# A hybrid encoder on one core: the first norm by square root and one Newton step, its first tiles reordered, and the last two tiles of the final norm woven

## The chip, the cores and the metric

The kernel runs on one core of a Trainium2 chip. The metric is the device time of one execution in microseconds (us); lower is better. Five engines work from queues of their own, each in order: TensorE (PE; its weight loads are listed as PEld), VectorE (DVE), ScalarE (ACT), GpSimd (POOL) and SyncE (SP, which here only issues transfers). Tiles lie in SBUF; TensorE writes its results to PSUM.

## The reference

Two layers work on 1024 tokens of width 1024. Layer 0 mixes by neighbourhood attention, layer 1 by grouped-query attention. Each layer then adds a gated per-layer embedding, and a last RMS norm ends the trunk.

```python
def rms_norm(x, g):
    xf = x.astype(jnp.float32)
    y = xf * lax.rsqrt(jnp.mean(xf * xf, axis=-1, keepdims=True) + NORM_EPS)
    return (y * g.astype(jnp.float32)).astype(x.dtype)

def reference(x, p, norm_g, ...):
    for i in range(DEPTH):                                  # DEPTH = 2
        h = rms_norm(x, norm_g[i])
        y = mixer_a(h, ...) if i % 2 == 0 else mixer_b(h, ...)
        x = x + y
        g = jax.nn.sigmoid(rms_norm(x, ple_norm_g[i]) @ ple_w_gate[i])
        x = x + g * (p[i] @ ple_w_proj[i])
    return rms_norm(x, final_norm_g)
```

`mixer_a` projects h to q, k, v and a gate, attends over a window of 8 rows x 16 columns with a learned bias, multiplies by silu(gate) and projects again. `mixer_b` does the like with normalised and rotated q and k over all tokens.

## The kernel before

**Tiles and numbers.** The 1024 tokens are eight tiles of 128 (`NT`). A product in float32 accuracy is three TensorE products: each operand is split in a high part and a low part (`wh`, `wl` for weights, `HTh`, `HTl` for the normalised and transposed tokens), and `split3` (through `mm`, line 305) adds high times high, high times low and low times high. The high part is an ACT copy, the low part a DVE subtraction.

**Weights.** `WQ` walks a list of units of 128 x 1024 numbers (512 KB). `stage` has SP issue the next load into one of two staging tiles `wstage` (line 203), as long as no more than two units are ahead of the split. `pump` copies the high part on ACT (line 220) and leaves the low part (line 221, DVE) to the next `settle`. At most `WSLOTS` = 4 split units live at a time. A pump that isn't forced waits for a few pumps after a load. The list begins with av0, av1 (the first quarter of V's weights), aqk0, aqk1.

**The start of layer 0** (`mixer_a`, the stretch behind `e2`). SP loads tile 0, the gain broadcast to all 128 partitions, tile 1, the two V units and tiles 2 to 7. For a tile t, `square(t)` (ACT, line 723) sums the squares, `newton` (DVE) makes the reciprocal root by an integer seed and three Newton steps, `scale(t)` multiplies the tile by root and gain (line 739 on DVE for tiles 0, 1, 2, 4, 6; lines 741 and 742 on ACT and POOL for 3, 5, 7), and `ht(t)` transposes it on TensorE in two halves of four blocks (line 430), which ACT copies to HTh (line 431) and DVE subtracts to HTl (line 432). `vs[t][0]` and `vs[t][1]` are the two halves of V's product for tile t, 12 matmuls each; ACT and DVE evacuate it (lines 590 and 591). The order of all that is written out by hand. Between t=0 and t=1, SP issues the mask and eight loads of the bias table into `U`; behind t=3, sixteen copies from `U` to `U2` (line 793). Then come the q and k products of head 0 (matmuls of 512 columns) and the attention loop, in which `mix` lays attention steps and dense products side by side by hand-set weights.

**The roots.** `rsqrt_ops` gives the list of tiny DVE operations of a reciprocal root: shift, multiply-add, a halving, and three Newton steps of two operations for one column or three for several. `newton`, `norms` and `finish_norm` (layer 1's q and k norms, spread over later slots by `post`) use it.

**The end** (`dense_phase(1)`, kind "ple", second half). For each tile, 24 matmuls of 512 columns fill a PSUM tile; `gated` takes tanh on ACT (line 1221) and two DVE operations (1222, 1223) that update X; ACT squares (1281); `norms` makes the root (414 and on), POOL scales the low half (419), DVE the high half (422), and SP stores the tile. The last tile is computed in two column halves (`halves`), its low half is scaled by ACT (421), and SP issues its two stores one after the other (1289, 1290). On DVE, `norms` of tile 6 comes before the `gated` operations of tile 7.

Of the kernel before, what the change touches and what calls it, by code (L numbers as in the profile page):

```python
# [11 lines left out]
F32 = mybir.dt.float32  # L12
# [9 lines left out]
NT = 8  # L22
KC = 8
# [4 lines left out]
BIG = 1e30  # L28
WSLOTS = 4
# [9 lines left out]
HOLD = 2  # L39
DP = 1  # L40
# [44 lines left out]
def lay_out(inp):  # L85
# [57 lines left out]
    def swap(v):  # L143
# [6 lines left out]
        "mask": mask, "rope": np.stack([cosT, sinT], axis=1),  # L150
    }
# [3 lines left out]
def trunk(ctx, tc, x, wts, rpb, gains, hgains, mask, rope, out):  # L155
# [21 lines left out]
    class Weights:  # L177
        def __init__(self):
# [13 lines left out]
            self.rest = None  # L192
            self.gate = None
# [13 lines left out]
        def pump(self, force=False):  # L207
# [13 lines left out]
            self.rest = lambda: dve.tensor_tensor(lo, s, hi, ALU.subtract)  # L221
# [90 lines left out]
    def rsqrt_ops(dst, ms, wk):  # L312
        n = dst.shape[1]
        mi = ms.bitcast(I32)
        y, a, h = wk[:, 0:n], wk[:, n:2 * n], wk[:, 2 * n:3 * n]
        yi = y.bitcast(I32)
        ops = [lambda: dve.tensor_scalar(yi, mi, 1, None, op0=ALU.logical_shift_right),
               lambda: dve.tensor_scalar(yi, yi, -1, 0x5F3759DF, op0=ALU.mult, op1=ALU.add),
               lambda: dve.tensor_scalar(h, ms, -0.5, None, op0=ALU.mult)]
        for i in range(3):  # L320
            to = dst if i == 2 else y
            if n == 1:
                ops += [lambda: dve.scalar_tensor_tensor(a, y, h, y, op0=ALU.mult, op1=ALU.mult)]
            else:
                ops += [lambda: dve.tensor_tensor(a, y, y, ALU.mult),
                        lambda: dve.tensor_tensor(a, a, h, ALU.mult)]
            ops += [lambda to=to: dve.scalar_tensor_tensor(to, a, 1.5, y, op0=ALU.add, op1=ALU.mult)]
        return ops

    def rsqrt(dst, ms, wk):  # L330
        for f in rsqrt_ops(dst, ms, wk):
            f()
# [50 lines left out]
    def proj_N(keys, t, ncol, alloc, evac, release=(), kstep=None):  # L383
# [5 lines left out]
        for k0, k1 in chunks(nk, kstep):  # L389
            def f(k0=k0, k1=k1):  # L390
                if k0 == 0:
                    st["ps"] = alloc()
                for k in range(k0, k1):
# [15 lines left out]
    def norms(sb, sq, ts, xns, xts, gt, final):  # L409
        n = len(ts)  # L410
        wk = sb.tile([128, 8], F32, name="wkn", bufs=2)
        st = sb.tile([128, 4], F32, name="stn", bufs=3)
        ms, r = st[:, 0:n], st[:, 2:2 + n]
        dve.scalar_tensor_tensor(ms, sq[:, 1, ts[0]:ts[0] + n], 1.0 / D, sq[:, 0, ts[0]:ts[0] + n], op0=ALU.mult, op1=ALU.add)
        rsqrt(r, ms, wk)
        for i in range(n):
            if final:
                if ts[i] < NT - 1:
                    pool.tensor_scalar(xns[i][:, :512], xts[i][:, :512], r[:, i:i + 1], None, op0=ALU.mult)
                else:  # L420
                    act.activation(xns[i][:, :512], xts[i][:, :512], AF.Copy, scale=r[:, i:i + 1])
                dve.scalar_tensor_tensor(xns[i][:, 512:], xts[i][:, 512:], r[:, i:i + 1], gt[:, 512:], op0=ALU.mult, op1=ALU.mult)
            else:
                dve.scalar_tensor_tensor(xns[i], xts[i], r[:, i:i + 1], gt, op0=ALU.mult, op1=ALU.mult)
# [138 lines left out]
    def mixer_a():  # L563
        with ExitStack() as es:
# [4 lines left out]
            psO = es.enter_context(tc.tile_pool(name="apo", bufs=2, space=PSUM))  # L569

# [14 lines left out]
            def v_items(qd, t):  # L585
# [6 lines left out]
                return [d[0] for d in proj_N(keys, t, 256, valloc, evac, release=keys if t == NT - 1 else ())]  # L592
# [119 lines left out]
            ini = e2.enter_context(tc.tile_pool(name="ini", bufs=1))  # L712
            X = [ini.tile([128, D], F32, name=f"X{t}") for t in range(NT)]
            gt = ini.tile([128, D], F32, name="gain")
# [10 lines left out]
            def newton(a, b):  # L725
                ms = stat[:, 1, a:b]
                return [lambda: dve.tensor_scalar(ms, stat[:, 0, a:b], 1.0 / D, EPS, op0=ALU.mult, op1=ALU.add)] \
                    + rsqrt_ops(stat[:, 2, a:b], ms, wk)

            def weave(ops, fs):  # L730
                per = -(-len(ops) // len(fs))
                for i, f in enumerate(fs):
                    for o in ops[i * per:(i + 1) * per]:
                        o()
                    f()

            def scale(t):
                if t % 2 == 0 or t == 1:
                    dve.scalar_tensor_tensor(X[t], X[t], stat[:, 2, t:t + 1], gt, op0=ALU.mult, op1=ALU.mult)
                else:  # L740
                    act.activation(X[t], X[t], AF.Copy, scale=stat[:, 2, t:t + 1])
                    pool.tensor_tensor(X[t], X[t], gt, ALU.mult)

            def ht(t):
                return [lambda c=c: to_ht(psT, t, X[t], (c,)) for c in range(2)]

            load(0)
            sync.dma_start(gt, bcast(gains, 0, D))
            load(1)
            WQ.stage(True)  # L750
            for t in range(2, NT):
                load(t)
            U = dram.tile([16, 8, 31, 24], F32, name="U")
            square(0)
            square(1)
# [19 lines left out]
            for t in range(1, NT):  # L775
# [3 lines left out]
                if t == 1:  # L779
                    square(7)  # L780
# [559 lines left out]
```

## Time and profile before

| | us |
|---|---|
| median of 3 runs (lowest to highest) | 1563.97 (1562.44 to 1564.62) |
| the profiled execution: its time | 1560.76 |
| its span, first to last instruction | 1558.9 |
| busy in it: TensorE / VectorE / ScalarE / GpSimd | 1519.0 / 1025.8 / 871.8 / 279.5 |

In the timeline a row has its start in us from the span's start, its duration, the engine, the line of the kernel, the operation, the tile written and the tiles read, their sizes and the count; a bracket gives the idle time of the engine just before it and what ended it. SPq is SyncE's transfer queue. Matmuls overlap, so the distance of two starts, not the duration, is what one costs.

### The profile page before, as it was taken

What the parts mean: (1) busy time and instruction counts of PE and PEld (TensorE: products, weight loads), DVE (VectorE), ACT (ScalarE), POOL (GpSimd) and SP (SyncE); (2) the same over time, 40 slices, a digit from 0 to 9 for tenths busy, and PEclk for the clock granted to TensorE, in tenths of its full rate; (3) what the DMA queues carried; (4) which work ended last, traced back from release to release, by engine and by line L of the source; (5) the groups of instructions that cost most, each with busy time, mean ns of one, the idle gap of its engine ahead of it and who ended that gap; (6) DMA issues with size and microseconds to landing.
All of it is one profiled execution on the core that took longest, in us unless ns stands there. A gap on an engine that the chain in (4) does not pass through costs nothing.

```text
span 1558.9 us, 24287 instructions
## 1 busy us (share of the span) xinstructions
PE 1519.0 (97%) x9048; PEld 1327.7 (85%) x9048; DVE 1025.8 (66%) x2062; ACT 871.8 (56%) x1744; POOL 279.5 (18%) x372
## 2 busy tenths in 40 slices
PE   6999999999999999999999999999999999999997
PEld 5888988988988788888988889989999888788886
DVE  6576477377477436648877787777877877625636
ACT  6465466376366622434466776766767777622422
POOL 2111121112112010000222132443131200000023
PEclk9999999999999999999999999999999999999999
DMA  8212122132122972142210111111111113651213
GB/s 274 78 41 75 44 89 79 35 95 82 35 85 83 336 260 68 54 141 94 76 49 21 39 38 55 45 38 50 56 33 42 61 55 117 225 200 54 75 55 128
DMA packets 89861, 138.84 MB, mean 89 GB/s; under 512 B 16912, under 2 KB 55952, under 8 KB 89744
## 3 DMA queue, kind: packets, MB, share of 16 engines
q1 hardware_dynamic: 85136, 122.62, 24.3%
q10 hardware_dynamic: 4608, 14.68, 2.6%
q8 instruction: 71, 1.16, 0.3%
q14 instruction: 46, 0.38, 0.1%
HBM read 104.65 MB, written 36.15 MB: 90 GB/s over the span
## 4 chain that ended last, share of the span: by engine, by line
PE 43%; DVE 6%; ACT 3%; issue 2%; ACTq 0%; DVEq 0%
PE d L305 23%; PE o L305 7%; PE t L1087 6%; PE s L305 6%; DVE PTl L1090 1%; DVE mn L1071 1%; ACT PTh L1089 1%; ACT P L1077 1%; PE t L430 1%; PE t L1041 0%; DVE QS L1051 0%; DVE wl L221 0%; DVE t L905 0%; DVE KB L982 0%; DVE qt L906 0%
## 5 line engine op out<-in xcount | busy, mean ns | idle before, releaser
L305 PE MATMUL d<-wh,HTh 128*128 128x256 f32 (+1 forms) x1096 | 372.6, 340 | 4.8 <-ACT HTh L431 2.1
L305 PE MATMUL d<-wh,HTl 128*128 128x256 f32 (+1 forms) x1096 | 365.9, 334 | 1.5 <-DVE HTl L432 1.5
L305 PE MATMUL d<-wl,HTh 128*128 128x256 f32 (+1 forms) x1096 | 365.2, 333 | 0.0
L1090 DVE TENSOR_TENSOR PTl<-t,PTh 128x512 fp32r<-128x512 f32 x256 | 164.5, 684 | 107.1 <-ACT PTh L1089 106.7
L305 PEld LDWEIGHTS d<-wh,HTh 128*128 128x128 f32 x1096 | 207.9, 190 | 28.2 <-ACT HTh L431 2.7
L305 PEld LDWEIGHTS d<-wh,HTl 128*128 128x128 f32 x1096 | 207.8, 190 | 24.0 <-DVE HTl L432 2.2
L305 PEld LDWEIGHTS d<-wl,HTh 128*128 128x128 f32 x1096 | 208.2, 190 | 21.4
L305 PE MATMUL d<-HTh,wh 128*128 128x512 f32 x504 | 206.0, 409 | 0.0
L305 PE MATMUL d<-HTh,wl 128*128 128x512 f32 x504 | 197.8, 392 | 0.0
L305 PE MATMUL d<-HTl,wh 128*128 128x512 f32 x504 | 197.7, 392 | 0.0
L1077 ACT ACTIVATE P<-s,mn 128x1024 f32<-128x1024 f32 x128 | 142.8, 1116 | 56.6 <-DVE mn L1071 55.7
L1089 ACT ACTIVATE PTh<-t 128x512 fp32r<-128x512 f32 x256 | 140.1, 593 | 45.8 <-PE t L1087 45.3
L1071 DVE TENSOR_REDUCE mn<-s 128x1 f32<-128x1024 f32 x128 | 154.9, 1210 | 11.9 <-PE s L305 11.8
L1087 PE MATMUL t<-ident,P 128*128 128x128 f32 x1024 | 136.9, 274 | 6.6 <-DVE PTl L1090 4.8
L221 DVE TENSOR_TENSOR wl<-wstage,wh 128x1024 fp32r<-128x1024 f32 x89 | 115.1, 1298 | 42.3 <-ACT wh L220 42.1
L305 PE MATMUL s<-KA,QS 128*128 128x512 f32 (+2 forms) x384 | 133.5, 402 | 0.0
L1087 PEld LDWEIGHTS t<-ident,P 128*128 128x128 f32 x1024 | 114.8, 140 | 21.7 <-DVE PTl L1090 15.8
L305 PE MATMUL s<-KB,QS 128*128 128x512 f32 (+2 forms) x384 | 121.8, 371 | 0.0
L305 PE MATMUL o<-PTh,V 128*128 128x256 f32 (+2 forms) x672 | 118.8, 287 | 1.5 <-DVE Y L446 0.9
L305 PE MATMUL o<-PTl,V 128*128 128x256 f32 (+2 forms) x672 | 119.3, 289 | 0.4 <-DVE PTl L684 0.3
L684 DVE TENSOR_TENSOR PTl<-t,PTh 128x384 fp32r<-128x384 f32 (+1 forms) x128 | 66.6, 521 | 76.1 <-ACT PTh L683 75.0
L305 PEld LDWEIGHTS d<-HTh,wl 128*128 128x128 f32 x504 | 94.6, 188 | 21.8
(179 smaller groups left out, 2483.6 us busy)
## 6 DMA issues: line engine op xcount, KB each, us to landing
wstage<-in_wts SPq DMA_DIRECT2D x92, 512.0 KB
X<-in_x SPq DMA_DIRECT2D x16, 512.0 KB
pp<-ppD SPq DMA_DIRECT2D x32, 256.0 KB
rb<-rD SPq DMA_DIRECT2D x56, 128.0 KB
ppD<-th SPq DMA_DIRECT2D x20, 256.0 KB
xD<-X SPq DMA_DIRECT2D x8, 512.0 KB
X<-xD SPq DMA_DIRECT2D x8, 512.0 KB
yD0h<-rb SPq DMA_DIRECT2D x14, 256.0 KB
```

The lines of the kernel that those rows point to most:

```text
L221: self.rest = lambda: dve.tensor_tensor(lo, s, hi, ALU.subtract)
L305: pe.matmul(ps, a, b, start=first, stop=last, skip_group_check=True)
L430: pe.transpose(ps[:, k], xn[:, (4 * c + k) * 128:(4 * c + k + 1) * 128], ident)
L684: dve.tensor_tensor(PTl[:, sl], ps[:, :m], PTh[:, sl], ALU.subtract)
L1071: dve.tensor_reduce(mn, ps, axis=AX.X, op=ALU.min)
L1077: act.activation(p, ps, AF.Exp, bias=mn, scale=-1.0, accum_out=RS[h, hf][:, t:t + 1])
L1087: pe.transpose(ps[:, i], p[:, k * 128:(k + 1) * 128], ident)
L1089: act.activation(PTh[:, ks, c], ps, AF.Copy)
L1090: dve.tensor_tensor(PTl[:, ks, c], ps, PTh[:, ks, c], ALU.subtract)
```

## The change

1. **Layer 0's norm.** `square(t)` is followed by a square root on ACT (`root`), a reciprocal on DVE and one Newton step, per tile. The gain comes as a 4 KB array laid out by the host (`gain0`, 128 x 8), loaded over ACT's queue and spread over the partitions by eight TensorE transposes into a PSUM tile `gain`. All scales run on DVE; tiles 0 and 1 in halves.
2. **Its order.** SP loads tile 0, av0, tile 1, av1, tiles 2 to 7. Sixteen transposes of the identity (`warm`) stand before and behind the eight that spread the gain. av0 is split ahead of tile 1's square; av1 and all later units until the end of this stretch have their low part made by POOL in four pieces. For tiles 0 and 1, V's matmuls are ordered by thirds (all high times high of a half first, and so on). Tile t+2 is scaled and tile t+3 squared inside tile t's turn. Forced pumps begin at t=4 instead of t=3. `psO` opens behind the stretch.
3. **Roots elsewhere.** `rsqrt_ops` takes half the mean square and makes the seed in one operation: two operations fewer.
4. **The end.** `last_tile` puts tile 7's first half ahead of tile 6's root on DVE, squares tile 7 by halves, scales tile 6's low half on ACT, and issues the two last stores from ACT's and SP's queues.

The diff, cut:

```diff
+SEED = 0x5F3759DF - (1 << 22) - (1 << 31)
+WARM = (8, 8)
+THIRDS = {0: ((0, 1, 2), (0, 2, 1)), 1: ((0, 1, 2), (0, 1, 2))}
...
-            self.rest = lambda: dve.tensor_tensor(lo, s, hi, ALU.subtract)
+            def rest(eng=self.low):
+                n = 1024 if eng is dve else 256
+                for c in range(0, 1024, n):
+                    eng.tensor_tensor(lo[:, c:c + n], s[:, c:c + n], hi[:, c:c + n], ALU.subtract)
+            self.rest = rest
...
-        ops = [lambda: dve.tensor_scalar(yi, mi, 1, None, op0=ALU.logical_shift_right),
-               lambda: dve.tensor_scalar(yi, yi, -1, 0x5F3759DF, op0=ALU.mult, op1=ALU.add),
-               lambda: dve.tensor_scalar(h, ms, -0.5, None, op0=ALU.mult)]
+        ops = [lambda: dve.tensor_scalar(y.bitcast(I32), hi, -0.5, SEED, op0=ALU.mult, op1=ALU.add)]
...
+                for n, i in enumerate(thirds[k0 // kstep] if thirds else ()):
+                    for k in range(k0, k1):
+                        ...
+                        a, b = ((HTh, wh), (HTh, wl), (HTl, wh))[i]
+                        mm(st["ps"], a[:, t, k, :], b[:, c], n == 0 and k == 0, n == 2 and k == nk - 1)
...
+            def root(t):
+                act.activation(wk[:, t:t + 1], stat[:, 0, t:t + 1], AF.Sqrt, scale=1.0 / D, bias=eps)
+
+            def newton(t):
+                ss, y, r = stat[:, 0, t:t + 1], stat[:, 1, t:t + 1], stat[:, 2, t:t + 1]
+                h, w = wk[:, 8 + t:9 + t], wk[:, 16 + t:17 + t]
+                dve.tensor_scalar(h, ss, -0.5 / D, -0.5 * EPS, op0=ALU.mult, op1=ALU.add)
+                dve.reciprocal(y, wk[:, t:t + 1])
+                dve.scalar_tensor_tensor(w, y, h, y, op0=ALU.mult, op1=ALU.mult)
+                dve.scalar_tensor_tensor(r, w, 1.5, y, op0=ALU.add, op1=ALU.mult)
+
+            def spread():
+                for k in range(KC):
+                    pe.transpose(gain[:, k * 128:(k + 1) * 128], gT[:, k:k + 1].to_broadcast([128, 128]), ident)
+
+            def scale(t, n=1024, cs=None):
+                for c in cs or range(0, 1024, n):
+                    dve.scalar_tensor_tensor(X[t][:, c:c + n], X[t][:, c:c + n], stat[:, 2, t:t + 1], gain[:, c:c + n],
+                                             op0=ALU.mult, op1=ALU.mult)
+
+            def warm(ps, n):
+                for k in range(n):
+                    pe.transpose(ps[:, k % 4 * 128:k % 4 * 128 + 128], ident, ident)
...
+            act.dma_start(gT, gain0)
             load(0)
-            sync.dma_start(gt, bcast(gains, 0, D))
+            WQ.stage(True)                     # av0
             load(1)
+            WQ.stage(True)                     # av1
...
+            dve.memset(eps, EPS)
+            act.activation(junk[:, :1], eps, AF.Sqrt)
+            warm(gain, WARM[0])
+            spread()
+            warm(pd.tile([128, 512], F32, name="d"), WARM[1])
             square(0)
+            root(0)
+            newton(0)
+            scale(0, 512)
+            split()                            # av0, low part on DVE
+            square(1); root(1); newton(1)
+            scale(1, 512, (0,)); ht(0, (0,)); scale(1, 512, (512,)); ht(0, (1,))
+            vs[0][0]()
+            WQ.low = pool
+            split()                            # av1, low part on POOL
+            square(2); root(2); ht(1); newton(2); scale(2)
+            square(3); root(3); vs[0][1](); newton(3)
+            vs[1][0](); ht(2); square(4); root(4); scale(3); vs[1][1](); newton(4)
             ...                                # mask, U
-            for t in range(1, NT):
+            for t in range(2, NT):
                 vs[t][0]()
                 if t + 1 < NT:
+                    ht(t + 1)
+                if t + 3 < NT:
+                    square(t + 3); root(t + 3)
+                if t + 2 < NT:
+                    scale(t + 2)
                 vs[t][1]()
+                if t + 3 < NT:
+                    newton(t + 3)
                 ...
-                WQ.pump(t > 2)
+                WQ.pump(t > 3)
...
+                    def last_tile(t, xn):
+                        ...
+                        for i, w in enumerate((slice(0, 256), slice(256, 512))):
+                            ...                # 24 matmuls
+                            gated(t, ps, w)
+                            if i == 0:
+                                r = norm_r(sb, sq, t - 1, 1)
+                                act.activation(x7[:, cs][:, w], X[t][:, cs][:, w], AF.Square, accum_out=s7)
+                            else:
+                                low_half(act, xn, X[t - 1], r)
+                                act.activation(x7[:, cs][:, w], X[t][:, cs][:, w], AF.Square, accum_out=sq[:, 1, t:t + 1])
+                                dve.scalar_tensor_tensor(sq[:, 0, t:t + 1], s7, 0.5 / D, sq[:, 0, t:t + 1],
+                                                         op0=ALU.mult, op1=ALU.add)
+                                high_half(xn, X[t - 1], r, gt)
+                                sync.dma_start(out[t - 1], xn)
+                        r = norm_r(sb, sq, t, 1)
+                        low_half(act, x7, X[t], r)
+                        act.dma_start(out[t, :, :512], x7[:, :512])
+                        high_half(x7, X[t], r, gt)
+                        sync.dma_start(out[t, :, 512:], x7[:, 512:])
```

171 lines of the change are left out of this document (86 added, 85 removed).

## The prediction, made blind

> **What bounds the kernel now.** I read the page's busy table first, then the windows view, the waits of TensorE in the first 50 us, and the timeline of the first 50 and the last 15 us. In the first two fences: busy us, share and count of an engine; then start:end, length, busy us (count) of PE, PEld, DVE, ACT and POOL, granted clock, DMA share and GB/s.
>
> ```profile
> PE 1519.0 (97%) x9048; PEld 1327.7 (85%) x9048; DVE 1025.8 (66%) x2062; ACT 871.8 (56%) x1744; POOL 279.5 (18%) x372
> ```
> ```profile
> 8.90:21.20 12.30, 10.38 (x52) 9.23 (x52) 10.44 (x31) 8.32 (x13) 0.55 (x1) 1.00 1.02 361
> 21.20:49.74 28.54, 24.88 (x204) 24.16 (x205) 18.68 (x36) 16.48 (x31) 10.26 (x8) 1.00 0.61 179
> 200.00:1510.00 1310.00, 1295.02 (x7756) 1131.81 (x7755) 871.36 (x1674) 747.36 (x1486) 229.61 (x319) 1.00 0.26 86
> ```
>
> TensorE is the bound: from 200 to 1510 us it idles 15 of 1310 us. Shorter VectorE chains there are worth almost nothing. What can be won lies at the two ends: before the first matmul stream is dense, and behind the last matmul. The next fence says what TensorE waited for while layer 0 was normalised, transposed and multiplied into V (8.9 to 49.74 us): total us, times, longest.
>
> ```profile
> PE t L430 <- DVE X L739: 10.8, 4, 8.9
> PE d L305 <- ACT HTh L431: 2.1, 2, 1.1
> PE d L305 <- DVE HTl L432: 1.5, 2, 1.3
> ```
>
> Transposes wait for the scaled tile X, matmuls for its two halves HTh and HTl. That is the part that the change reorders.
>
> **The change, part 1: layer 0's lead-in.** Timeline rows (start, duration, engine, line, what; in brackets idle before and releaser):
>
> ```profile
> 4.34 1.06 ACT L723 ACTIVATE junk<-X 128x1024 bf16<-128x1024 f32 x1 [2.34 <-DMA X<-in_x]
> 5.52 0.15 DVE L727 TENSOR_SCALAR stat<-stat 128x1 f32<-128x1 f32 x1 [5.52 <-ACT junk L723]
> 7.49 1.28 DVE L739 SCALAR_TENSOR_TENSOR X<-X,stat,gain 128x1024 f32<-128x1024 f32 x1
> 7.81 1.06 ACT L723 ACTIVATE junk<-X 128x1024 bf16<-128x1024 f32 x1 [2.32 <-DMA X<-in_x]
> 8.92 1.94 PE L430 MATMUL t<-ident,X 128*128 128x128 f32 x8 [8.92 <-DVE X L739]
> 10.12 1.23 DVE L221 TENSOR_TENSOR wl<-wstage,wh 128x1024 fp32r<-128x1024 f32 x1 [1.35 <-ACT wh L220]
> 10.30 1.06 ACT L220 ACTIVATE wh<-wstage 128x1024 fp32r<-128x1024 f32 x1 [0.21 <-DMA wstage<-in_wts]
> 11.27 1.07 ACT L431 ACTIVATE HTh<-t 128x512 fp32r<-128x512 f32 x2
> 21.26 1.07 PE L430 MATMUL t<-ident,X 128*128 128x128 f32 x8 [0.51 <-DVE X L739]
> 23.88 0.36 ACT L590 ACTIVATE V<-d 128x256 fp32r<-128x256 f32 x1
> 33.06 1.29 DVE L432 TENSOR_TENSOR HTl<-t,HTh 128x512 fp32r<-128x512 f32 x2 [1.10 <-ACT HTh L431]
> ```
>
> Root of tile 0: ten tiny DVE ops took 5.52 to 7.49, so 0.2 us each. The new one is one ACT square root and, behind it, three such ops (reciprocal and two more; the fourth runs beside the root). The trace has no square root: a 128x1 op can't exceed the 0.36 us of the 128x256 evacuation, and I take 0.3. 5.52 + 0.3 + 3 x 0.2 gives 6.45, a gain of 1.0.
>
> The 512 KB broadcast of the gain leaves SP's queue; its place behind X0 goes to the first weight unit, and X1 stays third (7.81 as now). Four KB of gain go over ACT's queue and eight PE transposes spread them into PSUM, in time if the little load lands by about 4.5 (X0's 512 KB landed at 4.34). With those weights in hand by about 6.4, midway between the two X, ACT copies wh before X1 arrives. From X1 on ACT is the queue that decides; I add starts to starts: square 1.2 (4.34 to 5.52), root 0.3, HTh of tile 0 1.05, second wh 1.0, square of tile 2 1.2, root 0.3, HTh of tile 1 1.05: 7.8 + 6.1 = 13.9. DVE then has one HTl half (0.7, from 1.29 for two) and four tiny ops (0.8): the scale of tile 2 starts at 15.4, lasts 1.28, and its transposes start at 16.8 instead of 21.26. **Gain 4.5.** The new order in thirds (high times high, then the others) fits under this: TensorE has tile 0's first half from about 9.9, and wl of the second unit, moved to POOL, can be had in quarters:
>
> ```profile
> 20.65 2.72 POOL L742 TENSOR_TENSOR X<-X,gain 128x1024 f32<-128x1024 f32 x1 [19.36 <-ACT X L741]
> ```
>
> Four quarters by this row are 2.7 (11.4 to 14.2); the block that reads them ends about 14.6, ahead of the 16.8. The nearest DVE row is 1.23, so the move costs at most 1.5 on that block, which is covered.
>
> **Part 2: tiles 2 to 7.** All scales now go to DVE. One round of the loop scale, transposes, HTh, HTl, next scale stands in the trace:
>
> ```profile
> 30.34 1.28 DVE L739 SCALAR_TENSOR_TENSOR X<-X,stat,gain 128x1024 f32<-128x1024 f32 x1
> 31.76 1.06 PE L430 MATMUL t<-ident,X 128*128 128x128 f32 x8 [1.04 <-DVE X L739]
> 34.26 1.28 DVE L739 SCALAR_TENSOR_TENSOR X<-X,stat,gain 128x1024 f32<-128x1024 f32 x1
> 49.62 0.28 PE L305 MATMUL d<-wh,HTl 128*128 128x256 f32 x1
> 49.74 0.40 PE L305 MATMUL d<-HTh,wh 128*128 128x512 f32 x1
> ```
>
> A round is 34.26 - 30.34 = 3.92. TensorE's own work for a tile is 24 matmuls 0.118 apart (49.62 to 49.74) and 8 transposes, 2.83 + 0.92 (the row's 1.06 less the last one's tail) = 3.75. I take 3.83 between them. From tile 2's transposes (16.8) five rounds are 19.2, then tile 7's transposes 0.9, half of tile 6 1.4 and tile 7 2.8: 41.1. Before, this stretch took 49.74 - 21.26 = 28.5, because the odd tiles went through ACT and POOL.
>
> Against that stands one transfer:
>
> ```profile
> 22.11 0.54 SPq L203 DMA_DIRECT2D wstage<-in_wts  x1
> 24.90 10.71 SPq L793 DMA_DIRECT2D U<-U  x16
> ```
>
> The fourth weight unit (aqk1) was issued at 22.11, ahead of the sixteen table copies. With the forced split now starting at t=4 and not t=3, its issue falls behind those copies. SP runs some 2.2 us earlier (it waited for wl, 10.12 + 1.23 = 11.35; now that op follows the first scale, 6.5 + 1.5 + 1.2 = 9.2), so the copies end at 35.6 - 2.2 = 33.4 and aqk1 lands about 3.6 later, as the first load did (4.34), at 37. ACT reaches that copy at about 35, after tile 5's evacuation and ahead of tile 7's HTh in its order; so HTh of tile 7 comes at 38.7 and TensorE loses some 1.1 us (bounds 0, if it lands by 36, to 2.5). V ends at 42.2 instead of 49.74: **minus 7.5**. The rest of the kernel is TensorE's, so this moves through.
>
> The clock. Matmul rows:
>
> ```profile
> 14.85 0.41 PE L305 MATMUL d<-wh,HTl 128*128 128x256 f32 x1
> 15.61 1.94 PE L430 MATMUL t<-ident,X 128*128 128x128 f32 x8 [0.35 <-DVE X L739]
> 18.32 0.28 PE L305 MATMUL d<-wh,HTl 128*128 128x256 f32 x1
> ```
>
> The granted clock reads 1.00 all along, yet a 128x256 matmul takes 0.41 us at 14.85 and 0.28 at 18.32, and eight transposes 1.94 at 15.61 and 1.07 at 21.26. The 3 us before the switch hold 1.9 us of transposes, so I count the 24 new warm-up transposes (three times 1.94, 5.8 us ahead of tile 0) as activity and have TensorE fast from the first matmul. If it stays slow until 18, three blocks of twelve matmuls take 2.6 each and not 1.4; the slack of 2.2 (14.6 to 16.8) covers most, and some 1 us is lost. Every further slow microsecond loses half of one: until 25, 4.5.
>
> The Trainium skill, "TensorE: Matmul & The Clock Gate", Part 4, says that transposes do not count as PE-busy for the clock gate. By that rule the warm-up would do nothing and the total would be 1 to 4.5 us longer; the 15.61 row just before the switch speaks against it, but does not rule it out.
>
> A second activation table. Square, copy, exponential and tanh all ran off one load:
>
> ```profile
> 0.71 1.28 ACT L723 ACT_TABLE_LOAD   x1 [0.71 <-PEq L1332]
> 64.84 0.51 ACT L672 ACTIVATE sp<-sp,mn 128x256 f32<-128x256 f32 x1 [0.99 <-DVE mn L663]
> 68.08 0.38 PE L680 MATMUL t<-ident,sp 128*128 128x128 f32 x2
> ```
>
> If the square root needs a table of its own, a load of 1.28 comes before the first exponential. ACT is free from 63.85 and the transposes that read the exponential start at 68.08: hidden, cost 0 (without that cover 0.3).
>
> **Part 3: shorter roots elsewhere.** Two tiny ops (0.4 us) fewer for each root. Between 200 and 1510 they run beside TensorE: 0, bounds -0.8 to +0.5 (one step of the q and k roots moves a slot).
>
> **Part 4: the last two tiles.**
>
> ```profile
> 1546.92 0.39 ACT L1221 ACTIVATE th<-d 128x256 f32<-128x256 f32 x1
> 1547.05 0.16 DVE L414 SCALAR_TENSOR_TENSOR stn<-sq 128x1 f32<-128x1 f32 x1 [0.91 <-ACT xn L1281]
> 1549.03 0.75 DVE L422 SCALAR_TENSOR_TENSOR xn<-X,stn,gain 128x512 f32<-128x512 f32 x1
> 1549.69 0.42 DVE L1222 SCALAR_TENSOR_TENSOR th<-th,pp 128x256 f32<-128x256 f32 x1
> 1549.74 0.38 ACT L1221 ACTIVATE th<-d 128x256 f32<-128x256 f32 x1 [2.44 <-PE d L305]
> 1552.57 0.16 DVE L414 SCALAR_TENSOR_TENSOR stn<-sq 128x1 f32<-128x1 f32 x1 [0.91 <-ACT xn L1281]
> 1554.54 0.75 DVE L422 SCALAR_TENSOR_TENSOR xn<-X,stn,gain 128x512 f32<-128x512 f32 x1
> 1555.70 0.42 SPq L1290 DMA_DIRECT2D out<-xn  x1
> ```
>
> Tile 7's first half was ready at 1547.3, but stood on DVE behind tile 6's root until 1549.69. Now it goes first (1547.35 to 1548.2), then tile 6's root (eight ops where ten took 1547.05 to 1549.03, so 1.7 us, to 1550.0), then the second half's two ops (1550.2 to 1551.0), a fold (0.2) and tile 6's high half (0.75) to 1552.0. ACT meanwhile scales tile 6 and squares the second half by 1551.7. Tile 7's root runs 1552.0 to 1553.7, both halves end at 1554.5, and the two stores go out together from ACT's and SP's queues instead of at 1555.3 and 1555.70. That is 1.2 earlier for the later store, less 0.2 as both move at once: **minus 1.0** (bounds -0.5 to -1.4).
>
> **Sum.** -7.5 - 1.0 = -8.5. The profiled execution took 1560.76 (span 1558.9), so 1552.3; it was 3.2 under the median of the runs, 1563.97. Against that median: 1555.5. Its own range is 1552.5 to 1558.5. No change within 0.2%, 3.1 us, can be told from noise.
>
> **The rivals.**
> - The clock stays slow. If TensorE is fast only at 25 us, -8.5 becomes -4.0: 1560.0. For it: the new matmuls come in short blocks with waits. Against it: the activity before 18 was as broken. Chance 0.10.
> - Transfers become the bound. The DMA share is 1.02 in the 8.9:21.2 row and SP's chain ends only 2.2 earlier. If aqk1 lands at 41, ACT is held 4 us more: 1559.5 to 1560.5. Against it: only one transfer is on the path. Chance 0.10.
> - The table thrashes (slower). If square is not in the square root's table, squares and roots of 8 tiles cost 16 loads of 1.28 on ACT, 20.5 us. ACT's round is then 2.9 (two HTh 1.05, square 1.2, root 0.3, evacuation 0.36) + 2.6 = 5.5 instead of 3.83, and the first three tiles, where ACT decides, pay 2.6 each: 5 x 1.7 + 3 x 2.6 = 16 less some slack, about +14, so 1555.5 + 14 = 1569.5. It is slower once loads cost over some 8.5 us on the path. Against it: square shared its table with everything else here. The Trainium skill, "ScalarE: Activation LUTs", section "Table sets: the hidden batching unit", says that cheap functions sit in every set as filler; no run here shows it for square. Chance 0.06.
> - The lead-in's gain isn't passed on, because some later wait holds the date: 1562.5. Against it: the windows from 49.74 on are full. Chance 0.06.
> - More is won: aqk1 in time, the loop at 3.75, inner roots worth 0.8: 1552. Chance 0.06.
>
> My forecast has 0.62. The range 1552.5 to 1561.0 takes in the clock and transfer cases. Faster: 0.62 and most of 0.10, 0.10 and 0.06, so 0.80; same 0.13; slower 0.07.
>
> **What would show it.** Right: tile 2's transposes near 16.8, the first 128x512 matmul near 42.2, one table load before the first exponential, a wait of ACT on the fourth weight unit near 35, the last stores issued near span minus 4. Wrong: table loads between squares and roots, 0.41 us matmuls after 18, TensorE waiting after 42 longer than before, or last stores apart.

## The result and the profile after

The changed kernel takes 1553.69 us, median of five runs (1551.52 to 1555.43), against 1562.44 for the kernel before on the same chip (1562.26 to 1564.62). The ratio is 0.9941, with a 95% interval of 0.9927 to 0.9954: 8.75 us faster, where the prediction had 8.5. The prediction's 1555.5 was counted from 1563.97, the median of three runs; over five runs that median is 1562.44, which makes 1.5 of the 1.8 us between 1555.5 and 1553.69. The two profiled executions took 1560.76 and 1551.52 us, with spans of 1558.9 and 1549.5, so the two profiles lie 9.4 us apart.

The page's busy table and the windows view of the changed kernel answer to the first fences of the prediction. The first window runs from the first transposes to tile 2's, the second on to the first matmul of 512 columns, where V is done.

```profile
PE 1520.9 (98%) x9072; PEld 1330.5 (86%) x9072; DVE 1014.4 (65%) x1987; ACT 872.2 (56%) x1754; POOL 283.2 (18%) x384
...
7.70:16.80 9.10, 7.90 (x53) 6.99 (x52) 8.20 (x19) 7.25 (x15) 2.81 (x4) 1.00 1.03 411
16.80:43.38 26.58, 25.31 (x205) 24.13 (x205) 18.91 (x44) 15.47 (x32) 6.74 (x11) 1.00 0.69 192
200.00:1510.00 1310.00, 1295.38 (x7753) 1132.92 (x7753) 865.14 (x1631) 743.50 (x1479) 231.95 (x319) 1.00 0.25 85
```

The same work of TensorE now lies in 9.1 + 26.6 us, where it lay in 12.3 + 28.5; the middle of the kernel is as full as it was. The waits of TensorE between 7 and 50 us have shrunk from 14.4 us to 2.3:

```profile
PE d L315 <- ACT HTh L444: 1.0, 1, 1.0
PE d L315 <- DVE HTl L445: 0.8, 2, 0.6
PE t L443 <- DVE X L755: 0.5, 1, 0.5
```

The timeline of the lead-in (root of tile 0, transposes of tiles 0, 1, 2, 3 and 7, the transfers on SP's queue, the split of the fourth weight unit, the first matmul behind it, and the end of V):

```profile
5.92 0.29 ACT L739 ACTIVATE wki<-stat,eps 128x1 f32<-128x1 f32 x1
7.76 1.97 PE L443 MATMUL t<-ident,X 128*128 128x128 f32 x8
12.10 1.34 PE L443 MATMUL t<-ident,X 128*128 128x128 f32 x8
16.84 1.06 PE L443 MATMUL t<-ident,X 128*128 128x128 f32 x8 [0.53 <-DVE X L755]
20.75 1.06 PE L443 MATMUL t<-ident,X 128*128 128x128 f32 x8
22.95 10.15 SPq L841 DMA_DIRECT2D U<-U  x16
33.22 2.96 SPq L208 DMA_DIRECT2D wstage<-in_wts  x2
36.43 1.06 PE L443 MATMUL t<-ident,X 128*128 128x128 f32 x8
38.33 1.06 ACT L225 ACTIVATE wh<-wstage 128x1024 fp32r<-128x1024 f32 x1 [2.90 <-DMA wstage<-in_wts]
39.92 0.39 PE L315 MATMUL d<-wh,HTh 128*128 128x256 f32 x1 [1.01 <-ACT HTh L444]
43.38 0.40 PE L315 MATMUL d<-HTh,wh 128*128 128x512 f32 x1
57.51 1.28 ACT L683 ACT_TABLE_LOAD   x1
```

Tile 2's transposes start at 16.84, 4.4 earlier than before. From there the rounds are 3.92 us each. The sixteen copies leave SP's queue at 33.1; aqk1 is issued behind them, and ACT stands 2.90 us for it, up to 38.33. That wait is the one that the prediction named, but longer. V ends at 43.38, 6.36 earlier than 49.74. There is a single table load for the square root's set (at 1.14, before the data) and one back at 57.51, and neither is on TensorE's path.

The end, from tile 7's last root operation on:

```profile
1544.92 0.16 DVE L334 SCALAR_TENSOR_TENSOR stn<-wkn 128x1 f32<-128x1 f32 x1
1545.11 0.72 ACT L432 ACTIVATE xn<-X,stn 128x512 f32<-128x512 f32 x1 [1.83 <-DVE stn L334]
1545.11 0.75 DVE L437 SCALAR_TENSOR_TENSOR xn<-X,stn,gain 128x512 f32<-128x512 f32 x1
1545.87 0.37 ACTq L1308 DMA_DIRECT2D out<-xn  x1
1545.94 0.33 SPq L1310 DMA_DIRECT2D out<-xn  x1
```

The two stores go out 0.07 us apart. From the last matmul's start to the span's end it is 8.4 us (1541.12 to 1549.5); before it was 9.5.

To see where else time went, I set TensorE's instructions of both traces side by side, matmul for matmul, and took the difference of their start times. The step at each place is what was won there:

| stretch (us of before) | won | |
|---|---|---|
| up to the end of V, 49.7 | 6.36 | predicted 7.5 |
| 527 to 536, end of layer 0's attention | -0.9 | not predicted |
| 735, and 765 to 850, layer 1's prologue | 0.2 + 1.1 | predicted 0 |
| 1405 to 1460 and 1505 to 1545, layer 1's dense phase | 1.35 | not predicted |
| everything else up to the last matmul | 0.2 | predicted 0 |
| behind the last matmul | 1.1 | predicted 1.0 |

These add up to 9.4, the difference of the spans. So the total was met, but three terms inside it were not: V's end fell short by 1.1, layer 1's prologue and the step at 735 gave 1.3, and its dense phase gave another 1.35.

### The profile page after: what moved, and what is told of

The parts are those of the page before. It is cut to its first block, busy times and chain, and to the rows that moved or that the text cites. A ratio compares the mean times of both kernels' runs of the same rounds, so it can differ in the third digit from the quotient of the medians.

```text
span 1549.5 us, 24284 instructions
## 1 busy us (share of the span) xinstructions
PE 1520.9 (98%) x9072; PEld 1330.5 (86%) x9072; DVE 1014.4 (65%) x1987; ACT 872.2 (56%) x1754; POOL 283.2 (18%) x384
## 4 chain that ended last, share of the span: by engine, by line
PE 43%; DVE 6%; ACT 2%; issue 2%; ACTq 0%; DVEq 0%
PE d L315 23%; PE o L315 7%; PE t L1137 6%; PE s L315 6%; DVE PTl L1140 1%; DVE mn L1121 1%; ACT PTh L1139 1%; ACT P L1127 1%; PE t L443 1%; PE t L1091 0%; DVE QS L1101 0%; DVE wl L230 0%; DVE t L955 0%; DVE qt L956 0%; DVE KB L1032 0%
## 5 line engine op out<-in xcount | busy, mean ns | idle before, releaser
L1139 ACT ACTIVATE PTh<-t 128x512 fp32r<-128x512 f32 x256 | 140.0, 593 | 45.2 <-PE t L1137 44.8
L230 DVE TENSOR_TENSOR wl<-wstage,wh 128x1024 fp32r<-128x1024 f32 x85 | 108.5, 1281 | 40.3 <-ACT wh L225 39.8
```

The source lines that it names most:

```text
L230: eng.tensor_tensor(lo[:, c:c + n], s[:, c:c + n], hi[:, c:c + n], ALU.subtract)
L1139: act.activation(PTh[:, ks, c], ps, AF.Copy)
```

## The experiments

Where a run is a single one, its time can't tell a microsecond from another, and the reading goes by its trace. The kernels before that were run beside these took 1561.8 to 1563.5.

**What the wait for aqk1 costs.** The fourth weight unit is issued ahead of the copies; nothing else is changed.

```diff
                 if t == 3:
+                    WQ.stage(True)
                     for r in range(16):
```

> The changed kernel, but the fourth weight unit (aqk1) is issued at t=3, ahead of the sixteen table copies. My theory: ScalarE's wait of 2.90 us for it goes (0 to 0.3 left), HTh of tile 7 starts near 37.1 and not at 39.29, and the first matmul of 512 columns moves from 43.38 to 41.6 (minus 1.8). Rival (the transfers as a whole are the bound): the wait moves to another load and the mark stays within 0.5 of 43.38.

One run: 1548.98 us. The timeline of this kernel, transposes of tile 0, split of aqk1, transposes of tile 7, end of V:

```profile
7.99 1.17 PE L443 MATMUL t<-ident,X 128*128 128x128 f32 x8
...
35.00 1.05 ACT L225 ACTIVATE wh<-wstage 128x1024 fp32r<-128x1024 f32 x1
36.10 1.06 PE L443 MATMUL t<-ident,X 128*128 128x128 f32 x8
41.30 0.40 PE L315 MATMUL d<-HTh,wh 128*128 128x512 f32 x1
```

ACT splits aqk1 at 35.00 with no wait, and V ends at 41.30 instead of 43.38, 2.1 earlier. Of that, 0.33 is there before the wait: tile 2's transposes start at 16.50 and tile 7's at 36.10, instead of 16.84 and 36.43. From tile 7's transposes to the end of V it is 5.2 us here and 6.95 in the changed kernel. So the wait cost 1.75 us, where the prediction had 1.1 with bounds of 0 to 2.5.

The first row tells of the clock, too. Before any matmul of V, eight transposes take 1.17 us here, where they take 1.97 in the changed kernel's own 7.76 row and 1.04 to 1.06 at full speed. TensorE had done nothing but transposes until then: the 16 warm-up ones, the eight that spread the gain, and these. So transposes alone did raise the clock. (In the run without thirds, below, the trace has the clock full from 7.69, before the first transpose of a tile at 7.90.) The Trainium skill, "TensorE: Matmul & The Clock Gate", Part 4, which says that they do not count as PE-busy in the same way, is contradicted by this row.

**Timed.** The same kernel, in five rounds.

> The changed kernel with the fourth weight unit alone issued ahead of the copies, timed in five rounds. Theory (the landing of that unit varies from run to run, and a long wait for it idles TensorE and halves the clock): a median near 1550 us and runs closer together than the 1551.5 to 1555.4 of the changed kernel. Rival (the single run at 1548.98 was luck): a median of 1553 to 1554 and the same spread.

Median 1550.92 us (1549.71 to 1552.56), ratio to before 0.9927 (0.9914 to 0.9939), so 2.8 below the changed kernel's median; the kernel before took 1562.72 beside it and 1562.44 beside the changed one. The two intervals overlap a little, so it is the trace that carries the cause: here too it is 5.2 us from tile 7's transposes to the end of V. The theory is borne out on the median and half on the spread: 2.9 us against 3.9. What spreads the rest isn't shown; two places that vary from run to run are named at the end of this section.

**Is the loop bound by the order of its three engines?** The scales of tiles 2 to 7 are made in two halves of 512, so that the transposes of the first half need not wait for the second.

```diff
-                    scale(t + 2)
+                    scale(t + 2, 512)             # also for tiles 2 and 3
```

> The changed kernel, but every scale of layer 0's norm is two operations of 512 columns, so that a tile's first transposes can start half a scale earlier. Theory (the loop of 3.92 us is the latency scale, transposes, HTh, HTl): the distance of one tile's transposes to the next's falls to TensorE's 3.75, tile 7's transposes start near 35.8 and not at 36.43; the first matmul of 512 columns stays near 43.4, since the wait for the fourth weight unit sets it. Rival (VectorE's work is the bound of the loop): the distance rises by 0.13, to 4.05.

One run: 1558.51 us, worse. Three of the five rounds did shrink to 3.74 (transposes at 20.26, 24.00, 27.74 and 31.48), so the price of 3.92 was DVE's whole scale in them. The first and the last round took 4.04, so all five together won only 0.3. But aqk1 landed late and the time went there:

```profile
31.48 1.04 PE L443 MATMUL t<-ident,X 128*128 128x128 f32 x8
40.62 1.06 ACT L225 ACTIVATE wh<-wstage 128x1024 fp32r<-128x1024 f32 x1 [6.26 <-DMA wstage<-in_wts]
42.22 0.58 PE L315 MATMUL d<-wh,HTh 128*128 128x256 f32 x1 [3.94 <-ACT HTh L444]
47.77 0.39 PE L315 MATMUL d<-HTh,wh 128*128 128x512 f32 x1
```

The windows view of that place (last numbers: granted clock, DMA share, GB/s):

```profile
30.00:38.28 8.28, 8.16 (x66) 7.52 (x64) 6.34 (x13) 3.48 (x8) 2.83 (x4) 1.00 0.91 273
38.28:40.90 2.62, 0.00 (x0) 0.00 (x0) 0.00 (x0) 0.28 (x1) 0.00 (x0) 1.00 0.75 280
40.90:47.70 6.80, 5.48 (x24) 5.26 (x25) 1.62 (x3) 2.02 (x4) 4.89 (x9) 0.50 0.25 88
```

Here is the price of a long wait: TensorE stands 3.94 us for HTh, which stands behind the split on ACT, and the granted clock falls to 0.50 for 6.8 us. The matmuls at 42.22 and behind it are the slow ones again. The wait of 6.3 us on ACT cost about 7 us: with these scales and the unit early, V ends at 40.81 (the run before the last in this section).

**Is the warm-up needed?** `WARM = (0, 0)`: the 16 transposes of the identity are left out; the eight that spread the gain stay.

> The changed kernel without the sixteen warm-up transposes; the eight that spread the gain stay. My theory (transposes count as activity): the fast matmuls (128x256 in 0.28 us) begin 2 to 8 us later than now, where they begin at 10.3; tile 2's transposes start 0.3 to 1.5 later than 16.84; the first matmul of 512 columns stays within 0.5 of 43.4, since the wait for the fourth weight unit hides up to 2.2 us. Rival (the skill's rule, transposes do not count): nothing moves, fast matmuls from the same time as now.

One run: 1552.84 us. The timeline's rows of the first 5 us of V:

```profile
7.58 1.97 PE L443 MATMUL t<-ident,X 128*128 128x128 f32 x8 [0.89 <-DVE X L755]
9.38 1.22 PE L315 MATMUL d<-wh,HTh 128*128 128x256 f32 x4
10.40 1.05 PE L315 MATMUL d<-wl,HTh 128*128 128x256 f32 x4
11.34 0.98 PE L315 MATMUL d<-wh,HTl 128*128 128x256 f32 x4
12.16 1.09 PE L443 MATMUL t<-ident,X 128*128 128x128 f32 x8
```

Four matmuls take 1.22 to 0.98 us here; at full speed they take 0.64. The clock comes up at 11.9 instead of 9.9; in the nine traces with the warm-up it came up anywhere from 7.7 to 10.2, so how much of the 2 us is the warm-up's, this one trace can't say. Yet tile 2's transposes start at 16.77 and V ends at 43.43, as in the changed kernel, though I had expected tile 2 at least 0.3 later. Even against the earlier clock of the first experiment (tile 2 at 16.50) the loss is 0.3. The warm-up seems to work, and is worth 0.3 us at most in this order.

**Is the square root what makes the loop shorter?** Its place is taken by the three Newton steps on DVE that the rest of the kernel uses.

```diff
-                act.activation(wk[:, t:t + 1], stat[:, 0, t:t + 1], AF.Sqrt, scale=1.0 / D, bias=eps)
...
-                ...                                   # reciprocal and one Newton step
+                dve.tensor_scalar(y, ss, 0.5 / D, 0.5 * EPS, op0=ALU.mult, op1=ALU.add)
+                rsqrt(r, y, wk[:, 2 * t:2 * t + 2])
```

> The changed kernel with layer 0's root made by the integer seed and three Newton steps on VectorE (eight tiny operations for each tile) and no square root on ScalarE. Theory (the root's length is on the path of the first three tiles and of the loop): tile 2's transposes start some 2.4 later, at 19.2; the loop is 0.4 longer, 4.3; tile 7's transposes at 40.6; first matmul of 512 columns near 45.5 (plus 2, the rest is hidden behind the wait for the fourth unit); one table load in the whole kernel. Rival (ScalarE alone decides, so fewer operations there help): tile 2's transposes no later than 16.8.

One run: 1558.27 us. Tile 2 at 19.93 and rounds of 4.32, much as expected; V ends at 49.75, 4.3 later than expected, no earlier than before the change. The cause stands in the timeline:

```profile
33.36 0.22 DVE L330 SCALAR_TENSOR_TENSOR wki<-wki,stat 128x1 f32<-128x1 f32 x1
33.61 0.16 DVE L334 SCALAR_TENSOR_TENSOR wki<-wki 128x1 f32<-128x1 f32 x1
...
36.97 2.81 POOL L230 TENSOR_TENSOR wl<-wstage,wh 128x256 fp32r<-128x256 f32 x4 [22.76 <-ACT wh L225]
37.48 0.15 DVE L326 TENSOR_SCALAR wki<-stat 128x1 int32<-128x1 int32 x1
37.67 0.73 DVE L330 SCALAR_TENSOR_TENSOR wki<-wki,stat 128x1 f32<-128x1 f32 x1
38.44 0.66 DVE L334 SCALAR_TENSOR_TENSOR wki<-wki 128x1 f32<-128x1 f32 x1
39.14 0.66 DVE L330 SCALAR_TENSOR_TENSOR wki<-wki,stat 128x1 f32<-128x1 f32 x1
```

While POOL makes the four quarters of a low part (36.97 to 39.78), three tiny operations take 0.66 to 0.73 us instead of 0.16 to 0.22, about as long as one of POOL's quarters, 0.70. The one that reads a single operand, at 37.48, stays at 0.15. The round to tile 7 takes 5.77 (transposes at 37.20 and 42.97), TensorE runs dry behind them for 1.2 and 0.4 us, and the clock falls to half from 43.2 to 46.6. The Trainium skill, "GPSIMD Engine Reference", section 1, names contention with DVE instructions that have two SBUF inputs; these rows agree, with a delay of 0.5 us for each. With the scales in halves the same is seen in the last round, the one of 4.04: two such operations, at 32.11 and 32.91, took 0.77 and 0.66 beside POOL's quarters.

**The thirds.** `THIRDS = {}`: tiles 0 and 1 go block by block, as the other tiles do.

> The changed kernel with V's matmuls of tiles 0 and 1 in the plain order (the three products of each block together). Theory (ScalarE's queue decides up to tile 2): tile 2's transposes stay within 0.3 of 16.84; the block that waits for the second unit's low part starts later, 0.5 to 1 us, inside the slack. Rival (TensorE decides there): tile 2's transposes 1 us later or more.

One run: 1554.93 us. Tile 2's transposes start at 17.17, 0.33 later, with the same rounds; V ends at about 46.0. But the clock came up at 7.69 here and at 9.89 in the changed kernel. Against the first experiment, whose clock came up at 8.25, tile 2 is 0.67 later. So the thirds are worth 0.3 to 0.7, a little more than expected. The rest of the loss is aqk1 again: ACT stood 3.67 us for it, up to 39.43, and the clock fell to half from 41.8 to 45.2.

**The low parts on POOL.** `WQ.low = pool` is left out, so the low parts of av1 and later units are made by DVE.

> The changed kernel with all low parts of the weights on VectorE (1.23 us each) and none on GpSimd. Theory: the second unit's low part stands on VectorE ahead of tile 1's HTl and tile 2's root, so tile 2's transposes start 0.6 to 1.2 later than 16.84; in the loop one 1.2 us operation at t=4 delays one round by 0.7 to 1.2. Rival (GpSimd's shared access slows VectorE's tiny operations, and that costs more than the moved work): tile 2's transposes no later than 16.9 and tile 7's no later than 36.5.

One run: 1559.74 us. I expected tile 2 some 0.6 to 1.2 later; it starts at 16.86, as in the changed kernel and 0.36 later than in the first experiment, whose clock came up at nearly the same time (8.25, here 7.99). DVE's 1.22 us fell largely where it waited for HTh. The loss came at the other end: the round to tile 7 took 4.45 (transposes at 36.99), ACT stood 4.73 us for aqk1, the clock fell to half from 42.1 to 48.9, and V ended at 48.0. The low part on DVE in front of tile 7's scale is worth 0.5; the rest is the same wait.

**The roots elsewhere, alone.** The kernel before, with only `rsqrt_ops` shortened.

> The kernel before with the shorter reciprocal roots alone (two operations fewer in each, everywhere; layer 0's order, its old gain and the old end stay). Theory: layer 1's prologue (770 to 850 us) wins the 1.1 to 1.3 us that the changed kernel shows there against the kernel before, since its q and k roots end one slot earlier; layer 0's start wins 0.2 to 0.5; the 527 to 545 us stretch, where the changed kernel lost 0.9, shows whether that loss is the change's (0 here) or the one profile's (0.5 to 1.2 here too). Rival (my prediction's own value): roots are worth 0 between 200 and 1510.

One run: 1562.82 us, against 1561.9 beside it; too close to tell by time. By the trace, its lead-in was 1.35 later than before, since the gain and the second tile landed later, which the edit can't touch; tile 0's scale stood 1.43 us for the gain:

```profile
8.56 1.28 DVE L737 SCALAR_TENSOR_TENSOR X<-X,stat,gain 128x1024 f32<-128x1024 f32 x1 [1.43 <-DMA gain<-in_gains]
```

Between 765 and 850 it wins 1.08, where the changed kernel wins 1.09, and both win another 0.2 at 735. The two kernels that keep the old roots (the end alone and the extra tile, below) win less than 0.1 there. The waits of TensorE between 740 and 850 us in the kernel before, and then in the changed one (the same in this run):

```profile
PE t L1087 <- DVE PTl L1090: 1.6, 1, 1.6
PE t L1041 <- DVE PTl L1090: 0.8, 2, 0.6
PE t L1041 <- POOL qt L939: 0.4, 1, 0.4
```
```profile
PE t L1137 <- DVE PTl L1140: 1.4, 1, 1.4
PE t L1091 <- DVE PTl L1140: 0.4, 2, 0.2
PE t L1091 <- POOL qt L989: 0.3, 1, 0.3
```

The roots of q and k stand on DVE ahead of the split of the first probabilities. The waits fall from 2.8 to 2.1. In the matmul for matmul comparison the steps are 0.45 at 777 us, 0.20 at 798 and 0.42 at 842, where a wait of 0.6 has gone. The listed waits account for 0.7 of the 1.1.

**The end, alone.** The kernel before, with only `last_tile`.

> The kernel before with the woven end alone (old roots). Theory: from the last matmul's start to the span's end 8.3 to 8.5 us, where the kernel before takes 9.5 and the changed kernel, whose roots are 0.25 us shorter twice, 8.4 less that: the end is worth 1.0 or less, the rest of the kernel moves by nothing but noise. Rival (the stores' own time is the bound and the weave hides nothing): 9.3 or more.

One run: 1560.75 us, against 1561.9. From the last matmul to the end it is 8.7 us, 0.8 less than before and a little more than the 8.3 to 8.5 expected; with the roots alone it was 9.0, 0.5 less. Together that is 1.3, and the change has 1.1. But this kernel also won 0.6 at 1405 to 1460 and 0.74 at 1505 to 1548, as the changed one does, and nothing in the end's instructions lies there.

**A tile of four bytes.** `last_tile` allocates one more tile, `s7`, of 4 bytes per partition. It moves the pool that holds the weights of the second half of layer 1's dense phase from the address 189344 to 189376 in each partition, from 32 bytes beyond a multiple of 64 to a multiple of 64. These are the addresses in the built program. To test that alone, the kernel before gets such a tile in the dense phase of both layers, and nothing else. Of what these matmuls read, only the weights move by it; the transposed tokens stay where they are.

```diff
+            dve.memset(sb.tile([128, 1], F32, name="pad", bufs=1), 0.0)
             WQ.alloc[2] = ...
```

> The kernel before, with one extra 4-byte tile allocated in the dense phase of both layers and nothing else. Theory (the address of the second-half weights, 32 bytes off a multiple of 64, slows the 512-column matmuls that read them as moving operand): the distance between those matmuls goes from 0.234 to 0.229 us in the second halves of both layers' dense phases; about 1.35 us less in layer 1 between 1405 and 1548 us, about 1.9 us less in layer 0 between 570 and 730 us, the span 3.2 us shorter than 1558.9 (about 1555.7). Rival (the 0.6 and 0.7 us won there in the changed kernel are noise or the granted clock): the distances stay at 0.234 and the span within 1 us of 1558.9.

One run: 1558.87 us, against 1562.72 for the kernel before; span 1557.1, not 1555.7. One group of the grouped view of TensorE between 1510 and 1530 us (layer 1, second half; busy us and mean ns of one), of the kernel before, the changed one, and the one with the extra tile:

```profile
L305 PE MATMUL d<-wl,HTh 128*128 128x512 f32 x29 | 11.5, 395 | 0.0
```
```profile
L315 PE MATMUL d<-wl,HTh 128*128 128x512 f32 x30 | 11.6, 388 | 0.0
```
```profile
L305 PE MATMUL d<-wl,HTh 128*128 128x512 f32 x30 | 11.6, 388 | 0.0
```

The mean of one matmul falls from 395 ns to 388 in this group, and from 395 to 392 and 394 in the two other groups of that stretch. The distance of two starts, which is what counts, is (as a median) 0.234 us in the kernel before and 0.229 with the tile, in the second halves of both layers' dense phases; in the changed kernel it is 0.229 in layer 1 and still 0.234 in layer 0. The matmul for matmul comparison gives 1.5 us in layer 0 and 1.6 in layer 1 for the extra tile. The expected 1.35 in layer 1 stands, and the 1.9 in layer 0 was high. The span won less than these 3 because 0.6 was lost at 520 to 545 us and 1.0 at 1310 to 1325 (both below). That the tile's 32 bytes are the cause is shown by this pair; that it is the multiple of 64 is my reading of two addresses, and other offsets weren't tried.

**Both mends of the lead-in.** The fourth unit early and the scales in halves together.

> The changed kernel with the fourth weight unit issued ahead of the copies and the scales of tiles 2 to 7 in two halves, without the extra tile in layer 0's dense phase. It parts the two things that e10 added to e11 (1550.92 to 1548.06). Theory (the halves win 0.4 to 0.8 in the lead-in, the address about 1.9 in layer 0's dense phase): first 128x512 matmul at 40.9, layer 0's 512-column matmuls back at 0.234, median about 1550.3. Rival (the gain is the shorter rounds' and the address is worth nothing): a median of 1548. Besides: if the store of the per-layer product holds ScalarE near 1300 us only by chance, its wait need not appear here.

Median 1549.65 us (1548.74 to 1550.92), ratio 0.9917 (0.9904 to 0.9931). V ends at 40.81, as expected, and layer 0's matmuls are back at 0.234.

**And the tile in layer 0.** The same with the four bytes in layer 0's dense phase.

> The changed kernel, with the fourth weight unit issued ahead of the sixteen copies, the scales of tiles 2 to 7 made in two halves, and the extra 4-byte tile in layer 0's dense phase as well. Theory: no wait of ScalarE on the staged weights, 3.74 us per tile, first 128x512 matmul at 40.6 us, no fall of the granted clock by 50 us, and about 1.9 us less in layer 0's dense phase: about 1547 us, ratio to before 0.990. Rival: without the wait the transfers bound the loop instead (the first 128x512 matmul at 41.3 or later), and the alignment is worth nothing: 1549 to 1550 us.

Median of four runs 1548.06 us (1547.33 to 1548.27), ratio 0.9906 (0.9891 to 0.9921). V ends at 40.87. Set against the trace without the tile, it wins 1.7 us between 523 and 740 and nothing before; a further 1.0 lies behind 740, in stretches that vary from trace to trace. By the medians the tile is worth 1.6, but these two kernels ran on different chips, and the two intervals overlap. The rival of the run before this one, that the address is worth nothing, falls by the distances of the matmuls. This is the fastest version: by the ratios to the kernel before, 0.35% (5.5 us) under the changed kernel.

Its span could have been shorter still. In layer 1's attention ACT waits for an earlier store of the per-layer product to leave its buffer, and TensorE for ACT:

```profile
1297.78 0.60 ACT L567 ACTIVATE th<-d 128x512 f32<-128x512 f32 x1 [2.49 <-DMA ppD<-th]
...
1299.04 0.66 PE L1138 MATMUL t<-ident,P 128*128 128x128 f32 x4 [0.47 <-ACT th L1094]
```

This cost about 1.4 us at 1302 to 1318. The traces with the roots alone, the end alone, the extra tile and both mends show the same wait of 2.2 to 2.6 us and a loss of 1.0 to 1.5 there; the kernel before had 0.7 of it, and the changed kernel and the timed one with the unit early had none. The end of layer 0's attention, 527 to 536 us, is a second such place. TensorE waits 1.2 us there for ACT's PTh in the changed kernel; in the timed run with the unit early it waits as long, and the clock is halved behind it, from 527.6 to 531.0, at a cost of 1.6. The 0.9 that the changed kernel loses there shows in the runs of the roots alone (0.65), of the end alone (0.4) and of the extra tile (0.6) as well, and all other traces lose 0.4 or more there too. So at least 0.4 of it is the luck of the one trace of the kernel before, and no loss that the change made. I read both as the luck of a run; what decides it stays open. They bound what one trace can say about a microsecond.

## Why the prediction was right, and where its terms were off

- **Tile 2 at 16.8.** 16.84. The square root took 0.29 (taken as 0.3), and ACT was done with its chain at 13.96 (predicted 13.9). But two misses cancel in that. Tile 1 landed earlier, so its square started at 7.23 and not at 7.81, which no step of the working had; and from there the chain took 6.7 us and not 6.1, since the HTh copies of tiles 0 and 1 stood longer, in part for transposes that still ran at the slow clock. That 16.8 came out to the tenth is luck; that ACT's queue decides is not. The move of the low part to POOL was covered, as said.
- **Rounds of 3.83.** 3.92. The bounds were TensorE's 3.75 and the row's own 3.92, and I took the middle for no reason that a row gave. As the scales in halves showed (3.74 in three rounds), DVE's whole scale set the round, so the row was the price. Five rounds: 0.4 us short.
- **1.1 us for aqk1.** 1.75. The wait, its place on ACT and what is queued behind it were as told. The term was mis-sized at one step, the landing. The copies left the queue at 33.1 (predicted 33.4), but aqk1 took 5.1 us from its issue and not the 3.6 of the first load of the kernel, which had no transfer ahead of it. In the four other traces in which ACT stood for it, it took 5.4 to 6.8. The bounds held the changed kernel's trace (0 to 2.5), but not those in which ACT stood 3.7 to 6.3 us: the landing varies, and where TensorE then idled for 1.8 us or more the clock fell too. So the rival "transfers become the bound", aqk1 at 41, nearly came true in two of the experiments (40.2 and 40.6, for 1559.74 and 1558.51 us). How much of the 3.9 us over which the changed kernel's own runs spread is due to that landing isn't shown.
- **The clock.** Full from 9.9, so the rival of a slow clock (1560.0) is out; without the warm-up it was full from 11.9, with tile 2 no later. The prediction was right to go by the 15.61 row and not by the rule on transposes.
- **The table.** One load for eight squares and eight roots, and one back at 57.51, hidden: the thrash (1569.5) is out. The Trainium skill, "ScalarE: Activation LUTs", "Table sets: the hidden batching unit", has cheap functions in every set. The trace agrees for the copy, which the page names, and the square, which it doesn't: no load stands between copies, squares and roots.
- **Roots elsewhere: 0.** 1.3 us, in the changed kernel and by themselves (1.1 in layer 1's prologue and 0.2 at 735), beyond the lower bound of -0.8. The step that failed: I read the stretch 200 to 1510 as full because 15 us of 1310 were idle. But 2.8 of those 15 lay in layer 1's prologue behind the very chain that was shortened.
- **The end: -1.0.** -1.1. Alone, the shorter roots give -0.5 and the order -0.8.
- **What wasn't in the sum.** 1.35 us from the address of a pool, which no step of the diff names.

So the total of 8.5 was met (8.75 by the medians, 9.4 by the profiles) since 1.35 of luck with an address and 1.3 of roots stand against 1.1 less in the lead-in and 0.9 lost at 527. The two mechanisms that the prediction summed were right, and its closeness is luck. Without those two gains it would have been about 1553.7 + 2.65 = 1556.3, still inside the range.

## What to carry to other kernels

When a forced load is moved behind other transfers in its queue, price its landing by its worst trace, not by its issue: the wait for it grows, and once it left TensorE idle for 1.8 us or more here, the clock added some microseconds. Put the one load that an in-order engine will stand for ahead of the bulk. And before calling a stretch full, list the few waits in it: a shortened chain pays exactly there.

## What the runs showed of the hardware

- Matmuls of 512 columns are 0.234 us apart when the weights that they stream lie 32 bytes off a multiple of 64, and 0.229 when they lie on one: 2%, 1.3 to 1.6 us per half of a dense phase. Only these two offsets were seen.
- A tile of four bytes moved the tiles allocated behind it by 32 bytes in these programs, so an edit elsewhere can change the speed of matmuls that it doesn't touch.
- After 2.6 us in which TensorE did nothing, the granted clock fell to 0.50 and stayed there for 6.8 us; behind a wait of 1.8 us (no thirds, 39 us) and behind waits of 1.3 and 0.3 us (unit early, timed, 525 us) it fell for 3.4 us, yet behind waits of 1.6 and 0.3 us (no thirds, 529 us) it did not. So the length of a wait alone doesn't decide it; what else does is open.
- Tiny DVE operations with two SBUF inputs took 0.66 to 0.73 us instead of 0.16 to 0.22 beside POOL's subtraction, in the kernel with three Newton steps; with one input 0.15 as ever.
